# Products that nobody reads at every norm and around the last stage's routing

## The chip, the cores and the metric

The kernel runs on one core of one Trainium2 chip. The metric is the device time of one execution in microseconds; times of before are the median of three runs. TensorE (PE in the profile) multiplies, ScalarE (ACT) and VectorE (DVE) and GpSimd (POOL) work on tiles, SyncE (SP) issues most DMAs. TensorE's products land in PSUM, in tiles of one bank each: 512 f32 values in each of 128 partitions.

## The reference, cut to what matters

Three transformer blocks run one after the other on x of 256 tokens by 1024 features, in f32. What the change touches is the norms and the routing:

```python
def layer_norm(x, g, b):                       # first block, twice
    mu = mean(x, -1); var = mean((x - mu)**2, -1)
    return (x - mu) * rsqrt(var + 1e-5) * g + b
def rms_norm(x, g):                            # everywhere else
    return x * rsqrt(mean(x * x, -1) + 1e-6) * g

x = layer_norm(alpha * x + m @ w_out, ln1_g, ln1_b)        # first block, then its peer_ffn
x = layer_norm(alpha * h + f + e, ln2_g, ln2_b)
# second block, two layers: a mixer and an mlp, each output normed, scaled and added to x
x = x + rms_norm(mixer(rms_norm(x, g0)), g1)
x = x + rms_norm(mlp(rms_norm(x, g2)), g3)
# third block: mLSTM, SwiGLU, hgrn, mixture of experts, each behind a modulated rms_norm; a final rms_norm
top_logits, top_idx = top_k(t @ router_w, 2)               # the routing
top_w = softmax(top_logits)
y = sum over e of gates[:, e:e+1] * swiglu(t, wg[e], wu[e], wd[e])
```

## The kernel before

x stays in SBUF as a tile of 128 partitions by 8 slices by 256 tokens: features lie on partitions (slice k holds features 128k to 128k+127), tokens on the free axis. Every large product is made of three products of two-part values (`mm3`, lines L330 to L332): weights arrive by DMA, ACT rounds them to a part `hi` (L319) and DVE takes the rest `lo` (L320); inputs are split alike into pairs such as `nhi`, `nlo`. One such product is 128x256, in the trace as `128*128 128x256`, and its results gather in PSUM tiles named `mm` and `ac`. There are three pools of PSUM tiles: `mm` (two banks), `ac` (four) and `ms` (two); `ms` serves the norms and other small things.

A norm goes in a chain over several engines:

- Squares: ACT squares x by pairs of slices (L560, L564), DVE or POOL adds the tiles up (L568). The result is two tiles `sq`.
- `fold` (L497) multiplies them with a column of ones on TensorE: eight f32 products 128x1, in the trace 16 records of L371, into a bank `ms` ("the sums").
- `rstd` (from L373): ACT takes the root from that bank (`rs_t`, L379), DVE reads the same bank (`rs_v`, L380) and makes the reciprocal root in four more steps on 128x2 tiles (`rs_r`, L381 to L384).
- `rstd_rows` (L402) calls `spread` (L389): two f32 products 128x128 with the identity (four records of L394) put the 256 values on every partition, into the other bank `ms`.
- A reader takes the spread: DVE's `yk` in `layer_norm` (L456) and `rms` (L418), ACT's copy `rsb` in `add_normed` (L478), DVE's `x` at the end (L1987). From there ACT makes the rounded part (`lhi` L457, `nhi` L422 or L494), and the next stage's wide products can begin.

The norms are called at eleven places: twice `layer_norm` (first block); `add_normed` four times (second block: three times with `g`, where it prepares the next stage's input as well, and once without); `rms` through `modulated` three times in the third block (mLSTM, SwiGLU, hgrn); `Router.finish` for the routing (it uses `fold` and `rstd` but not `rstd_rows`); and the final norm (L1987). Where x is centred for a layer norm, its mean comes from `rows_add` (L400), f32 products 128x256.

The routing (`Router.finish` and `places`): ACT copies the logits to SBUF, TensorE transposes them (two products, L1795), DVE forms `lg` (L1797), takes the top values and their places (L1816, L1817), the masks `mk` (L1821); TensorE counts (L1824, L1825 and, for the largest count, L1840); DVE makes slots and the selectors `pm` (L1876); TensorE gathers the tokens of an expert (L1883), and the experts' products follow (L1908 on). Beside this chain, DVE and ACT make the normed tokens `xt` (L1804) and their parts `xhi`, `xlo` (L325, L326).

The program is written in order, and a scheduler places each engine's instructions; an instruction waits by semaphores for those on other engines whose tiles it needs.

Of the kernel before, what the change touches and what calls it, by code (L numbers as in the profile page):

```python
# [22 lines left out]
T = 256  # L23
# [194 lines left out]
class Core:  # L218
# [180 lines left out]

        self.nc.tensor.matmul(ps, self.C("onesD"), x, start=first, stop=last)  # L400

    def rstd_rows(self, sums, eps):  # L402
        return self.spread(self.ms_ps()[:, :T], self.rstd(sums[:, :2], eps))

    def squares(self, x):
        s = Squares(self)
# [1 line left out]
            s.add(x[:, 2 * j:2 * j + 2])  # L408
        return s

    def rms(self, x, sums, g, b=None, eps=1e-6):

        nc = self.nc
        r = self.rstd_rows(self.fold(sums), eps)
        hi, lo = self.big([KT, T], F32R, nm="nhi"), self.big([KT, T], F32R, nm="nlo")
        for k in range(KT):
            y = self.small([T], tag="yk", bufs=3)
            nc.vector.scalar_tensor_tensor(y, x[:, k], g[:, k:k + 1], r, op0=OP.mult, op1=OP.mult)  # L418
            if b is None:
                self.split(y, hi[:, k], lo[:, k])  # L420
            else:
                nc.scalar.activation(hi[:, k], y, AF.Identity, bias=b[:, k:k + 1])  # L422
                nc.vector.scalar_tensor_tensor(lo[:, k], y, b[:, k:k + 1], hi[:, k], op0=OP.add, op1=OP.subtract)
        return hi, lo
# [11 lines left out]
    def layer_norm(self, r, mean, g, b, g_next=None):  # L436


        nc = self.nc
        sq = Squares(self, nc.vector)  # L440
        for k in range(KT):
            nc.vector.tensor_tensor(r[:, k], r[:, k], mean, op=OP.subtract)
            if k % 2:
                sq.add(r[:, k - 1:k + 1])
        gh, bh = g, b
        if g_next is not None:
            gh, bh = (self.small([KT], tag=t, bufs=1) for t in ("gh", "bh"))
            nc.gpsimd.tensor_tensor(gh, g, g_next, op=OP.mult)
            nc.gpsimd.tensor_tensor(bh, b, g_next, op=OP.mult)
        rs = self.rstd_rows(self.fold(sq), 1e-5)  # L450
        hi, lo = (self.big([KT, T], F32R, nm="lhi"), self.big([KT, T], F32R, nm="llo"))
        sq = Squares(self)
        for k in range(KT):
            y = self.small([T], tag="yk", bufs=3)
            c = slice(k, k + 1)
            nc.vector.tensor_tensor(y, r[:, k], rs, op=OP.mult)  # L456
            nc.scalar.activation(hi[:, k], y, AF.Identity, scale=gh[:, c], bias=bh[:, c])  # L457
            eng = nc.vector if k < LNV else nc.gpsimd
            eng.tensor_scalar(r[:, k], y, g[:, c], b[:, c], op0=OP.mult, op1=OP.add)
            if g_next is None:  # L460
                nc.vector.tensor_tensor(lo[:, k], r[:, k], hi[:, k], op=OP.subtract)
            else:
                nc.vector.scalar_tensor_tensor(lo[:, k], r[:, k], g_next[:, c], hi[:, k], op0=OP.mult, op1=OP.subtract)
                if k % 2:
                    sq.add(r[:, k - 1:k + 1])
        return sq, (hi, lo)
# [4 lines left out]
    def add_normed(self, x, src, gm, sq, g=None):  # L471

        nc = self.nc
        r = self.rstd_rows(self.fold(sq), 1e-6)
        rs = self.small([T], tag="rsb", bufs=1)
        nc.scalar.activation(rs, r, AF.Copy)  # L478
        nxt = Squares(self, None if g is not None else nc.vector)
        parts = (self.big([KT, T], F32R, nm="nhi"), self.big([KT, T], F32R, nm="nlo")) if g is not None else None  # L480
        for k in range(KT):
            m = self.small([T], tag="yk", bufs=3)
            nc.vector.scalar_tensor_tensor(m, src(k), gm[:, k:k + 1], rs, op0=OP.mult, op1=OP.mult)
            eng = nc.vector if k < ADDS else nc.gpsimd
            eng.tensor_tensor(x[:, k], x[:, k], m, op=OP.add)
            if g is not None:
                self.scaled(x, k, g, parts)
            if k % 2:
                nxt.add(x[:, k - 1:k + 1])
        return nxt, parts  # L490
# [3 lines left out]
        self.nc.scalar.activation(hi, x[:, k], AF.Copy, scale=g[:, k:k + 1])  # L494
        self.nc.vector.scalar_tensor_tensor(lo, x[:, k], g[:, k:k + 1], hi, op0=OP.mult, op1=OP.subtract)  # L495

    def fold(self, sq):  # L497

        ps = self.sums()
        n = len(sq.tiles)  # L500
        for i, t in enumerate(sq.tiles):
            for f in range(2):
                self.add_sum(ps, 0, t[:, f], i + f == 0, i == n - 1 and f == 1, square=False)
        return ps
# [906 lines left out]
        nc.vector.tensor_tensor(self.mod[:, l, o:o + 16], cols, c.V(f"ada_b{l}")[:, o:o + 16], op=OP.add)  # L1411


def modulated(c, x, sums, w, scale, shift, out=None):
    nc = c.nc
    g = c.small([KT], tag="mg")
    nc.vector.scalar_tensor_tensor(g, scale, 1.0, w, op0=OP.add, op1=OP.mult)
    if out is None:
        return c.rms(x, sums, g, shift)
    return c.rms_whole(x, sums, g, shift, out=out)  # L1420


# [207 lines left out]
def hgrn(c, x, sums, mod):  # L1630
# [2 lines left out]
    nc.scalar.dma_start(lev, d["levels"])  # L1633
    masks = lev[:, :1024].bitcast(I32).rearrange("p (a b) -> p a b", a=8)
    reset = lev[:, 1024:1280]
    hs = modulated(c, x, sums, c.V("n1w1"), mod[:, 1, 8:16], mod[:, 1, 0:8])
    f, q = c.big([KT, T], nm="hf"), c.big([KT, T], nm="hq")
    P = lambda j: c.lin_chunk(d["h_in"][j], hs)
    for j in range(4):
# [3 lines left out]
    for j in range(2):  # L1643
        w = slice(4 * j, 4 * j + 4)
# [76 lines left out]
    v, g = c.big([2, D], nm="hv"), c.big([KT, T], nm="hg")  # L1721
# [11 lines left out]
    sq = {}  # L1733
# [17 lines left out]
class Router:  # L1751
# [35 lines left out]
    def finish(self, sq):  # L1787
        c, nc = self.c, self.c.nc
        r = c.rstd(c.fold(sq)[:, :2], 1e-6)
        lt = c.small([T], tag="lt", bufs=1)  # L1790
        nc.scalar.activation(lt[:8], self.lg, AF.Copy)
        pt = c.ac_ps()[:, :16].rearrange("p (a e) -> p a e", a=2)
        lg = c.small([2, 8], tag="lg", bufs=1)
        for tt in range(2):
            nc.tensor.transpose(pt[:, tt], lt[:8, tt * 128:tt * 128 + 128], c.C("ident")[:8, :8])  # L1795
        for tt in range(2):
            nc.vector.scalar_tensor_tensor(lg[:, tt], pt[:, tt], r[:, tt:tt + 1], self.bias, op0=OP.mult, op1=OP.add)  # L1797
        found = places(c, lg)
        parts = (c.big([2, D], F32R, nm="xhi"), c.big([2, D], F32R, nm="xlo"))
        for tt in range(2):  # L1800
            for a in range(0, D, 512):
                w = slice(a, a + 512)
                t = self.xt[:, tt, w]
                nc.vector.scalar_tensor_tensor(t, t, r[:, tt:tt + 1], self.row[:, w], op0=OP.mult, op1=OP.add)  # L1804
                c.split(t, parts[0][:, tt, w], parts[1][:, tt, w])
        return parts, found


def places(c, lg):

    nc = c.nc
    top, tf, mk = (c.hold([2, 8], t) for t in ("top", "tf", "mk"))
    ti = c.hold([2, 8], "ti", U32)
    oh = c.hold([2, 2, 8], "oh")
    for tt in range(2):
        nc.vector.max(top[:, tt], lg[:, tt])  # L1816
        nc.vector.max_index(ti[:, tt], top[:, tt], lg[:, tt])  # L1817
    nc.vector.tensor_copy(tf, ti)
    nc.vector.tensor_tensor(oh, c.C("iota")[:, None, None, :8].to_broadcast([128, 2, 2, 8]),
                            tf[:, :, 0:2, None].to_broadcast([128, 2, 2, 8]), op=OP.is_equal)  # L1820
    nc.vector.tensor_tensor(mk, oh[:, :, 0], oh[:, :, 1], op=OP.add)  # L1821
    ps = c.ms_ps()[:, :32]
    both = mk.rearrange("p a e -> p (a e)")
    nc.tensor.matmul(ps[:, 0:16], c.C("upto"), both, start=True, stop=False, skip_group_check=True)  # L1824
    nc.tensor.matmul(ps[:, 8:16], c.C("one"), mk[:, 0], start=False, stop=True, skip_group_check=True)  # L1825
    slot, gt = (c.hold([2, 8], t) for t in ("slot", "gt"))
    nc.vector.tensor_tensor(slot, mk, ps[:, 0:16].rearrange("p (a e) -> p a e", a=2), op=OP.mult)
    nc.vector.tensor_scalar(slot, slot, -1.0, None, op0=OP.add)

    w = c.hold([2, 4], "w")  # L1830
    nc.vector.tensor_tensor(w[:, :, 1:2], top[:, :, 1:2], top[:, :, 0:1], op=OP.subtract)
    nc.scalar.activation(w[:, :, 1:2], w[:, :, 1:2], AF.Exp)
    nc.vector.tensor_scalar(w[:, :, 2:3], w[:, :, 1:2], 1.0, None, op0=OP.add)
    nc.vector.reciprocal(w[:, :, 0:1], w[:, :, 2:3])
    nc.vector.tensor_tensor(w[:, :, 1:2], w[:, :, 1:2], w[:, :, 0:1], op=OP.mult)
    nc.vector.tensor_tensor(oh, oh, w[:, :, 0:2, None].to_broadcast([128, 2, 2, 8]), op=OP.mult)
    nc.vector.tensor_tensor(gt, oh[:, :, 0], oh[:, :, 1], op=OP.add)
    ps = c.ms_ps()[:, :8]
    for tt in range(2):
        nc.tensor.matmul(ps, c.C("one"), mk[:, tt], start=tt == 0, stop=tt == 1)  # L1840
    most = c.hold([1], "most")
    nc.vector.tensor_reduce(most, ps, axis=AX.X, op=OP.max)
    mosti = c.hold([1], "mosti", I32)
    nc.vector.tensor_copy(mosti, most)
    return slot, gt, mosti
# [177 lines left out]
```

## Time and profile before

| | us |
|---|---|
| median of three runs (lowest, highest) | 3037.54 (3036.64, 3039.58) |
| the profiled execution | 3037.25 |
| its span in the trace | 3035.1 |
| TensorE busy | 2847.2 (94%) |
| VectorE busy | 2120.3 (70%) |
| ScalarE busy | 1580.2 (52%) |
| GpSimd busy | 271.9 (9%) |
| mean granted clock of TensorE, share of full | 0.959 |

A row of a timeline gives the start and the duration of an instruction (or of several alike in a row, x16), both in us, its engine, its line, its operation with what it writes and reads, and in brackets how long the engine had been idle before it and whose work ended that. A busy time sums records; TensorE's records overlap, so a row of several gives their whole extent. PEclk is the granted clock as a share of full speed: 1.00 is 2.4 GHz and 0.50 is 1.2 GHz; a value between them is a mean over a stretch that has both.

### The profile page before, as it was taken

What the parts mean: (1) busy time and instruction counts of PE and PEld (TensorE: products, weight loads), DVE (VectorE), ACT (ScalarE), POOL (GpSimd) and SP (SyncE); (2) the same over time, 40 slices, a digit from 0 to 9 for tenths busy, and PEclk for the clock granted to TensorE, in tenths of its full rate; (3) what the DMA queues carried; (4) which work ended last, traced back from release to release, by engine and by line L of the source; (5) the groups of instructions that cost most, each with busy time, mean ns of one, the idle gap of its engine ahead of it and who ended that gap; (6) DMA issues with size and microseconds to landing.
All of it is one profiled execution on the core that took longest, in us unless ns stands there. A gap on an engine that the chain in (4) does not pass through costs nothing. (4 is left out here: it accounts for less than half of the span.)

```text
span 3035.1 us, 52257 instructions
## 1 busy us (share of the span) xinstructions
PE 2847.2 (94%) x21378; PEld 2707.3 (89%) x21378; DVE 2120.3 (70%) x3619; ACT 1580.2 (52%) x2233; POOL 271.9 (9%) x176
## 2 busy tenths in 40 slices
PE   8799967899999999999999999999999999999998
PEld 8698966899999999988799988999899998788886
DVE  6365998976666667577655655555655596899997
ACT  5254534654444444436644455445544565777775
POOL 0000372200000000021000100000100062000000
PEclk9899988999999999999999999998999999999999
DMA  7544333477877788443155423543245442688885
GB/s 260 180 149 159 142 124 128 170 274 287 289 263 280 280 292 305 170 144 128 56 182 188 145 99 139 181 168 139 85 167 183 160 141 97 249 316 336 321 333 220
DMA packets 117712, 601.77 MB, mean 198 GB/s; under 512 B 9688, under 2 KB 45016, under 8 KB 48472
## 3 DMA queue, kind: packets, MB, share of 16 engines
q1 hardware_dynamic: 78480, 557.96, 50.5%
q10 hardware_dynamic: 38984, 40.39, 4.4%
q8 instruction: 170, 2.79, 0.4%
q14 instruction: 78, 0.64, 0.1%
HBM read 578.91 MB, written 19.39 MB: 197 GB/s over the span
## 5 line engine op out<-in xcount | busy, mean ns | idle before, releaser
L320 DVE TENSOR_TENSOR lo<-raw,hi 128x1024 fp32r<-128x1024 f32 x915 | 1123.5, 1244 | 601.6 <-ACT hi L319 598.4
L319 ACT ACTIVATE hi<-raw 128x1024 fp32r<-128x1024 f32 x955 | 1002.7, 1057 | 1021.1 <-PE mm L331 534.1
L330 PE MATMUL mm<-lhi,hi 128*128 128x256 f32 x1344 | 388.2, 289 | 5.5 <-ACT r L930 3.1
L332 PE MATMUL mm<-lhi,lo 128*128 128x256 f32 x1344 | 388.1, 289 | 3.6 <-DVE lo L320 3.5
L330 PE MATMUL mm<-nhi,hi 128*128 128x256 f32 x1312 | 378.8, 290 | 10.2 <-ACT nhi L494 6.8
L331 PE MATMUL mm<-llo,hi 128*128 128x256 f32 x1344 | 388.2, 289 | 0.0
L331 PE MATMUL mm<-nlo,hi 128*128 128x256 f32 x1312 | 379.0, 289 | 0.5 <-DVE nlo L495 0.5
L332 PE MATMUL mm<-nhi,lo 128*128 128x256 f32 x1312 | 376.8, 288 | 0.0
L330 PE MATMUL ac<-r,hi 128*128 128x256 f32 x1024 | 294.2, 288 | 0.7 <-ACT r L325 0.7
L331 PE MATMUL ac<-r,hi 128*128 128x256 f32 x1024 | 293.4, 287 | 0.0
L332 PE MATMUL ac<-r,lo 128*128 128x256 f32 x1024 | 293.2, 286 | 0.0
L330 PEld LDWEIGHTS mm<-lhi,hi 128*128 128x128 f32 x1344 | 262.3, 195 | 7.9 <-ACT r L930 3.7
L330 PEld LDWEIGHTS mm<-nhi,hi 128*128 128x128 f32 x1312 | 258.0, 197 | 12.3 <-ACT nhi L494 7.6
L332 PEld LDWEIGHTS mm<-lhi,lo 128*128 128x128 f32 x1344 | 262.5, 195 | 5.7 <-DVE lo L320 4.7
L331 PEld LDWEIGHTS mm<-llo,hi 128*128 128x128 f32 x1344 | 262.2, 195 | 1.1 <-issue 0.7
L331 PEld LDWEIGHTS mm<-nlo,hi 128*128 128x128 f32 x1312 | 257.9, 197 | 2.5 <-DVE nlo L495 1.7
L332 PEld LDWEIGHTS mm<-nhi,lo 128*128 128x128 f32 x1312 | 257.8, 197 | 0.1
L330 PEld LDWEIGHTS ac<-r,hi 128*128 128x128 f32 x1024 | 198.8, 194 | 0.9 <-ACT r L325 0.9
L331 PEld LDWEIGHTS ac<-r,hi 128*128 128x128 f32 x1024 | 198.8, 194 | 0.0
L332 PEld LDWEIGHTS ac<-r,lo 128*128 128x128 f32 x1024 | 198.3, 194 | 0.0
L331 PE MATMUL ac<-hlo,hi 128*128 128x256 f32 x688 | 193.0, 281 | 0.0
L330 PE MATMUL ac<-hhi,hi 128*128 128x256 f32 x688 | 192.8, 280 | 0.0
(591 smaller groups left out, 6253.6 us busy)
## 6 DMA issues: line engine op xcount, KB each, us to landing
raw<-in_moe_gu SPq DMA_DIRECT2D x88, 1024.0 KB, 5.9
raw<-in_peer_u SPq DMA_DIRECT2D x64, 1024.0 KB, 5.3
raw<-in_peer_v SPq DMA_DIRECT2D x64, 1024.0 KB, 4.9
raw<-in_ada SPq DMA_DIRECT2D x48, 1024.0 KB, 6.1
raw<-in_moe_d SPq DMA_DIRECT2D x40, 1024.0 KB, 5.9
raw<-in_up SPq DMA_DIRECT2D x32, 1024.0 KB, 4.9
raw<-in_down SPq DMA_DIRECT2D x32, 1024.0 KB, 4.9
raw<-in_ffn_gu SPq DMA_DIRECT2D x22, 1024.0 KB, 4.9
```

Of the source, the lines that this page charges most:

```text
L319: nc.scalar.activation(hi, raw[:, a:a + m], AF.Copy)
L320: eng.tensor_tensor(lo, raw[:, a:a + m], hi, op=OP.subtract)
L330: mm(ps, w[0], x[0], start=start, stop=False, **k)
L331: mm(ps, w[0], x[1], start=False, stop=False, **k)
L332: mm(ps, w[1], x[0], start=False, stop=stop, **k)
```

## The change

A new helper `busy(ps, n)` makes n f32 products of the identity with the first 256 columns of the constants, into columns 256 to 511 of the bank `ps`. Nothing reads these columns. In the trace each is a product `128*128 128x256` in f32. It is called:

- in `rstd_rows`: three into the bank of the sums, behind `rstd`, and `more` into the spread's bank, behind the spread: three by default, five in `add_normed` with `g`, sixteen in `add_normed` without;
- in `fold`, ahead of its products, `wait` of them: nine in both layer norms, seven at the hgrn norm, none elsewhere;
- in `Router.finish`: nine behind the two transposes, in their bank; in `places`: five behind L1840's products, in their bank.

These are 118 products in all.

```diff
+    def busy(self, ps, n):
+        for _ in range(n):
+            self.nc.tensor.matmul(ps[:, 256:512], self.C("ident"), self.cst[:, 0:256], start=True, stop=True)
+
-    def rstd_rows(self, sums, eps):
-        return self.spread(self.ms_ps()[:, :T], self.rstd(sums[:, :2], eps))
+    def rstd_rows(self, sums, eps, more=3):
+        r = self.rstd(sums[:, :2], eps)
+        self.busy(sums, 3)
+        ps = self.ms_ps()
+        self.spread(ps[:, :T], r)
+        self.busy(ps, more)
+        return ps[:, :T]
...
-    def rms(self, x, sums, g, b=None, eps=1e-6):
+    def rms(self, x, sums, g, b=None, eps=1e-6, wait=0):
...
-        r = self.rstd_rows(self.fold(sums), eps)
+        r = self.rstd_rows(self.fold(sums, wait), eps)
...
-        rs = self.rstd_rows(self.fold(sq), 1e-5)
+        rs = self.rstd_rows(self.fold(sq, 9), 1e-5)
...
-        r = self.rstd_rows(self.fold(sq), 1e-6)
+        r = self.rstd_rows(self.fold(sq), 1e-6, 16 if g is None else 5)
...
-    def fold(self, sq):
+    def fold(self, sq, wait=0):
...
         ps = self.sums()
+        self.busy(ps, wait)
...
-    hs = modulated(c, x, sums, c.V("n1w1"), mod[:, 1, 8:16], mod[:, 1, 0:8])
+    hs = modulated(c, x, sums, c.V("n1w1"), mod[:, 1, 8:16], mod[:, 1, 0:8], wait=7)
...
-        pt = c.ac_ps()[:, :16].rearrange("p (a e) -> p a e", a=2)
+        bank = c.ac_ps()
+        pt = bank[:, :16].rearrange("p (a e) -> p a e", a=2)
...
             nc.tensor.transpose(pt[:, tt], lt[:8, tt * 128:tt * 128 + 128], c.C("ident")[:8, :8])
+        c.busy(bank, 9)
...
-    ps = c.ms_ps()[:, :8]
+    bank = c.ms_ps()
+    ps = bank[:, :8]
     for tt in range(2):
         nc.tensor.matmul(ps, c.C("one"), mk[:, tt], start=tt == 0, stop=tt == 1)
+    c.busy(bank, 5)
```

Below stands the scheduler's order at three places. The first is TensorE at the `add_normed` without `g`: L371 is the fold, L394 the spread, L406 the new products; `ms_` with a number is one bank's tile, and the brackets name the engines whose semaphores an instruction waits for. Before:

```order
L371 MATMUL ms_21417<-cst,sq_3037_21414 128x1 [waits Activation_49]
L371 MATMUL ms_21417<-cst,sq_3037_21414 128x1
L394 MATMUL ms_21426<-cst,rs_r_21428 128x128 [waits DVE_49]
L394 MATMUL ms_21426<-cst,rs_r_21428 128x128
L371 MATMUL ms_21483<-cst,sq_3046_21446 128x1 [waits DVE_49,PE_49]
```

With the change:

```order
L371 MATMUL ms_21471<-cst,sq_3037_21468 128x1 [waits Activation_49]
L371 MATMUL ms_21471<-cst,sq_3037_21468 128x1
L406 MATMUL ms_21471<-cst 128x256 [waits DVE_49]
L406 MATMUL ms_21471<-cst 128x256 x2
L394 MATMUL ms_21492<-cst,rs_r_21481 128x128 [waits DVE_49]
L394 MATMUL ms_21492<-cst,rs_r_21481 128x128
L406 MATMUL ms_21492<-cst 128x256 x16
L371 MATMUL ms_21556<-cst,sq_3046_21519 128x1 [waits DVE_49,PE_49]
```

Three products stand now between the last fold and the spread, in the fold's bank, the first of them with a wait for DVE; sixteen stand behind the spread, in its bank, ahead of the next norm's fold. At the other `add_normed` it is the same with five in place of sixteen. ACT's copy `rsb`, which reads the spread, waits for TensorE in both programs; its wait is set at the last of the sixteen (or five), where before it was set at the spread's last product.

The second place is TensorE at the SwiGLU norm, where products of the hgrn norm's call stand too (bank `ms_25287` is that of the hgrn norm's sums). Before:

```order
L371 MATMUL ms_23046<-cst,sq_3284_23037 128x1
L394 MATMUL ms_23055<-cst,rs_r_23057 128x128 [waits DVE_49,PE_49]
L394 MATMUL ms_23055<-cst,rs_r_23057 128x128
L330 MATMUL mm_23117<-nhi_23067,hi_23109 128x256 [waits Activation_49]
L330 MATMUL mm_23181<-nhi_23067,hi_23173 128x256
L331 MATMUL mm_23117<-nlo_23068,hi_23109 128x256 [waits DVE_49]
```

With the change:

```order
L371 MATMUL ms_23125<-cst,sq_3284_23116 128x1
L406 MATMUL ms_23125<-cst 128x256 [waits DVE_49]
L406 MATMUL ms_23125<-cst 128x256 x2
L394 MATMUL ms_23146<-cst,rs_r_23135 128x128 [waits DVE_49,PE_49]
L394 MATMUL ms_23146<-cst,rs_r_23135 128x128
L406 MATMUL ms_23146<-cst 128x256 x3
L406 MATMUL ms_25287<-cst 128x256 [waits PE_49]
L406 MATMUL ms_25287<-cst 128x256 x2
L330 MATMUL mm_23202<-nhi_23152,hi_23194 128x256 [waits Activation_49]
L330 MATMUL mm_23266<-nhi_23152,hi_23258 128x256
L406 MATMUL ms_25287<-cst 128x256
L331 MATMUL mm_23202<-nlo_23153,hi_23194 128x256 [waits DVE_49]
```

Behind the spread and its three products stand three of the seven that the hgrn norm's `fold` calls for, and a fourth after two wide products. The other three stand at the hgrn norm, right ahead of its fold.

The third place is DVE at the routing: `lg` are the logits (L1797 before, L1811 with the change), `mk` the masks (L1821, now L1835), `xt` and `xlo` the normed tokens and their second parts. Before:

```order
L1804 SCALAR_TENSOR_TENSOR xt_26640<-xt_26640,rs_r_26973,shift_26641 128x512 [waits DVE_49,Pool_49]
L1797 SCALAR_TENSOR_TENSOR lg_26984<-ac_26983,rs_r_26973,rbias_26663 128x8 [waits PE_49]
L1797 SCALAR_TENSOR_TENSOR lg_26984<-ac_26983,rs_r_26973,rbias_26663 128x8
L1816 MAX top_26989<-lg_26984 128x8 [waits DVE_49]
...
L1804 SCALAR_TENSOR_TENSOR xt_26640<-xt_26640,rs_r_26973,shift_26641 128x512
L1819 TENSOR_TENSOR oh_26993<-cst,tf_26990 128x32 [waits DVE_49]
L1804 SCALAR_TENSOR_TENSOR xt_26640<-xt_26640,rs_r_26973,shift_26641 128x512
L1821 TENSOR_TENSOR mk_26991<-oh_26993 128x16 [waits DVE_49]
```

With the change:

```order
L1818 SCALAR_TENSOR_TENSOR xt_26738<-xt_26738,rs_r_27071,shift_26739 128x512 [waits DVE_49,Pool_49]
L1818 SCALAR_TENSOR_TENSOR xt_26738<-xt_26738,rs_r_27071,shift_26739 128x512
L1818 SCALAR_TENSOR_TENSOR xt_26738<-xt_26738,rs_r_27071,shift_26739 128x512 [waits Activation_49]
L326 TENSOR_TENSOR xlo_27136<-xt_26738,xhi_27135 128x512 [waits PE_49,Activation_49]
L326 TENSOR_TENSOR xlo_27136<-xt_26738,xhi_27135 128x512 [waits Activation_49] x2
L1818 SCALAR_TENSOR_TENSOR xt_26738<-xt_26738,rs_r_27071,shift_26739 128x512
L1811 SCALAR_TENSOR_TENSOR lg_27082<-ac_27081,rs_r_27071,rbias_26761 128x8 [waits PE_49]
L1811 SCALAR_TENSOR_TENSOR lg_27082<-ac_27081,rs_r_27071,rbias_26761 128x8
L1830 MAX top_27096<-lg_27082 128x8 [waits DVE_49] x2
...
L326 TENSOR_TENSOR xlo_27136<-xt_26738,xhi_27135 128x512 [waits Activation_49]
L1832 CAST tf_27097<-ti_27099 128x16 [waits DVE_49]
L1833 TENSOR_TENSOR oh_27100<-cst,tf_27097 128x32 [waits DVE_49]
L1835 TENSOR_TENSOR mk_27098<-oh_27100 128x16 [waits DVE_49]
```

Before, one `xt` stood ahead of `lg`, and three `xt` and two `xlo` between `lg` and `mk`; now four `xt` and three `xlo` stand ahead of `lg`, and one `xlo` between the two. `lg` waits for TensorE in both; now its wait is set at the ninth of the new products behind the transposes.

## Rows read from the trace of the kernel before

**Rows 1.** The page's busy times of the engines (us, share of the span, instructions) and the granted clock of TensorE in 40 equal slices of the span, in tenths.

```profile
PE 2847.2 (94%) x21378; PEld 2707.3 (89%) x21378; DVE 2120.3 (70%) x3619; ACT 1580.2 (52%) x2233; POOL 271.9 (9%) x176
...
PEclk9899988999999999999999999998999999999999
```

**Rows 2.** The waits of TensorE over the whole span: which operation waited for whom, us in total, how many times, the longest in us.

```profile
PE ms L371 <- DVE sq L568: 18.2, 4, 7.3
PE ms L394 <- DVE rs_r L384: 13.3, 10, 2.2
```

**Rows 3.** The timeline of TensorE at the second layer norm: the means' products (L400), the fold (L371), the spread (L394); start and duration in us.

```profile
1308.44 3.62 PE L400 MATMUL ms<-x,cst 128*128 128x256 f32 x16
1315.98 2.50 PE L371 MATMUL ms<-cst,sq 128*128 128x1 f32 x16 [3.92 <-DVE sq L568]
1319.68 1.22 PE L394 MATMUL ms<-cst,rs_r 128*128 128x128 f32 x4 [1.20 <-DVE rs_r L384]
```

**Rows 4.** The timeline of all engines at the first `add_normed` with `g`; start and duration in us.

```profile
1496.09 1.05 PE L371 MATMUL ms<-cst,sq 128*128 128x1 f32 x8 [0.52 <-ACT sq L560]
...
1497.47 0.16 DVE L380 TENSOR_SCALAR rs_v<-ms 128x2 f32<-128x2 f32 x1 [0.45 <-ACT rs_t L379]
...
1498.35 1.22 PE L394 MATMUL ms<-cst,rs_r 128*128 128x128 f32 x4 [1.21 <-DVE rs_r L384]
1499.61 0.38 ACT L478 ACTIVATE rsb<-ms 128x256 f32<-128x256 f32 x1 [2.16 <-PE ms L394]
...
1501.83 0.58 PE L330 MATMUL mm<-nhi,hi 128*128 128x256 f32 x1 [2.27 <-ACT nhi L494]
```

**Rows 5.** Stretches of TensorE: from and to in us, length, busy us and instructions, granted clock, share of the DMA engines and GB/s. First three places where the new products go (behind `rs_v` at the first and the third `add_normed` with `g`, and at the final norm), then the stretches of wide products behind the first and the second layer norm, the second `add_normed`, the mLSTM norm, the SwiGLU norm, the hgrn norm, and the gather behind the routing.

```profile
1497.70:1499.60 1.90, 1.22 (x4) 0.59 0.82 224
1841.10:1842.50 1.40, 0.71 (x4) 1.00 0.74 164
3026.90:3028.70 1.80, 1.19 (x4) 0.50 0.00 0
300.00:303.30 3.30, 3.30 (x14) 0.50 0.00 0
1322.10:1327.30 5.20, 5.20 (x23) 0.50 0.00 2
1699.70:1702.80 3.10, 3.10 (x14) 0.50 0.00 0
2058.40:2064.60 6.20, 6.20 (x28) 0.50 0.00 0
2204.50:2208.00 3.50, 3.50 (x15) 0.50 0.12 52
2403.30:2409.30 6.00, 6.00 (x27) 0.50 0.42 162
2593.20:2597.10 3.90, 3.90 (x18) 0.50 0.00 0
```

**Rows 6.** The timelines of all engines at the other three `add_normed` (second and third with `g`, the one without): their spreads.

```profile
1696.16 1.22 PE L394 MATMUL ms<-cst,rs_r 128*128 128x128 f32 x4 [1.20 <-DVE rs_r L384]
...
1841.77 0.71 PE L394 MATMUL ms<-cst,rs_r 128*128 128x128 f32 x4 [1.21 <-DVE rs_r L384]
...
2043.08 0.71 PE L394 MATMUL ms<-cst,rs_r 128*128 128x128 f32 x4 [2.15 <-DVE rs_r L384]
```

**Rows 7.** The timelines of TensorE at the folds of the first layer norm, the mLSTM norm, the SwiGLU norm (its second half, and the first wide product behind that norm) and the hgrn norm.

```profile
292.97 3.46 PE L371 MATMUL ms<-cst,sq 128*128 128x1 f32 x16 [3.98 <-DVE sq L568]
...
2051.10 3.54 PE L371 MATMUL ms<-cst,sq 128*128 128x1 f32 x16 [7.32 <-DVE sq L568]
...
2199.79 1.05 PE L371 MATMUL ms<-cst,sq 128*128 128x1 f32 x8 [1.06 <-ACT sq L560]
...
2204.44 0.79 PE L330 MATMUL mm<-nhi,hi 128*128 128x256 f32 x2 [1.11 <-ACT nhi L422]
...
2396.15 3.54 PE L371 MATMUL ms<-cst,sq 128*128 128x1 f32 x16 [3.03 <-DVE sq L568]
```

**Rows 8.** The timelines of TensorE some 10 us behind the first and the third `add_normed` with `g`, at the next fold there.

```profile
1510.30 1.05 PE L371 MATMUL ms<-cst,sq 128*128 128x1 f32 x8 [0.44 <-POOL sq L568]
...
1854.22 0.94 PE L371 MATMUL ms<-cst,sq 128*128 128x1 f32 x7 [1.98 <-POOL sq L568]
```

**Rows 9.** The timeline of TensorE at the routing: the transposes of the logits and the first products of the gather.

```profile
2584.36 0.38 PE L1795 MATMUL ac<-cst,lt 8*128 8x8 f32 x2
...
2593.17 0.77 PE L1883 MATMUL ac<-pm,xhi 128*128 128x256 f32 x2 [2.17 <-DVE pm L1876]
```

**Rows 10.** The timeline of DVE at the routing.

```profile
2584.78 0.36 DVE L1797 SCALAR_TENSOR_TENSOR lg<-ac,rs_r,rbias 128x8 f32<-128x8 f32 x2 [0.49 <-PE ac L1795]
...
2587.47 0.75 DVE L1804 SCALAR_TENSOR_TENSOR xt<-xt,rs_r,shift 128x512 f32<-128x512 f32 x1
...
2588.90 0.17 DVE L1821 TENSOR_TENSOR mk<-oh 128x16 f32<-128x16 f32 x1
```

**Rows 11.** The chain of waits that ended last, in order of time: start and duration in us, what; here the fold and the spread of the final norm.

```profile
3022.73 3.59 PE ms L371 x16
...
3027.51 1.24 PE ms L394 x4
```

More of the change, by code (lines that the diff above doesn't have):

```diff
@@ L1411, in finish, with modulated @@
         nc.vector.tensor_tensor(self.mod[:, l, o:o + 16], cols, c.V(f"ada_b{l}")[:, o:o + 16], op=OP.add)
-def modulated(c, x, sums, w, scale, shift, out=None):
+def modulated(c, x, sums, w, scale, shift, out=None, wait=0):
     nc = c.nc
@@ L1418, in modulated @@
     if out is None:
-        return c.rms(x, sums, g, shift)
+        return c.rms(x, sums, g, shift, wait=wait)
     return c.rms_whole(x, sums, g, shift, out=out)
```

## The prediction, made before the changed kernel ran

> **What bounds the kernel now.** I read the page's shares first, then the waits of TensorE, then the timelines of the places that the diff touches. TensorE is busy for 94% of the span, and its granted clock is at full speed in most slices [rows 1]. So time is won or lost in two ways only: TensorE stands still, or it runs at its lower level. The norms are where both happen. The ten waits of the spread (L394) for DVE's `rs_r` are 13.3 us together, and the fold's four waits (L371) for DVE's `sq` are 18.2 us [rows 2]. A norm is a serial chain: fold, ACT and DVE on 128x2 tiles, spread, a reader of the spread (ACT's `rsb` or DVE's `yk`), ACT's `nhi`, and only then wide products. At the first norm of the two-mixer block, `rs_v` ends at 1497.63, the spread starts at 1498.35 and takes 1.22 us, `rsb` starts 0.04 us after it, and TensorE has its next wide product at 1501.83, after 2.27 us idle [rows 4]. **What stands between the spread and its reader is therefore on the path in full.** One more thing is in these rows: `rs_v` waits 0.45 us for ACT's `rs_t`, though both only read the bank of the sums and take nothing from each other [rows 4]. In this kernel two engines that touch one PSUM bank are put in order, whatever columns they touch.
>
> The clock falls in the norms' waits. It was 0.50 (1.2 GHz) in seven stretches right behind a norm or the routing, with TensorE busy throughout; they lasted 3.3, 5.2, 3.1, 6.2, 3.5, 6.0 and 3.9 us, and then it was at 2.4 GHz [rows 5]. A slow stretch costs half its length, so these cost 1.65, 2.6, 1.55, 3.1, 1.75, 3.0 and 1.95 us. That is all that a kept clock could give back behind these places.
>
> **The price of one unread product.** The rows have its shape: L400 is eight f32 products 128x256 (two records each), 3.62 us [rows 3], so 0.43 us each at the full clock. At 1.2 GHz no row shows it; I take twice that.
>
> **Part 1: three products in the sums' bank, n behind the spread.** The three can start once `rs_v` has read the bank, and the spread comes behind them: 3 x 0.43 = 1.30 us, where 0.72 us pass now [rows 4]. That is 0.58 us late. The spread then runs at 0.71 us, as where the clock is at 1.00 [rows 5, 6], and not at 1.22: 0.51 earlier where it was slow. The n products behind it are in the reader's bank and stand ahead of the reader in the program; in the built order the reader's wait is set at the last of them. So the reader is late by 0.07 + 0.43n where the spread was slow, and by 0.58 + 0.43n where it was fast:
> - n = 3 (two layer norms, three pre-norms of the last stage, final norm): 1.37 us;
> - n = 5 (three add_normed with g): 2.2 us in the first two, 2.75 in the third, whose spread is at 0.71 already [rows 6];
> - n = 16 (add_normed without g): 0.58 + 6.9 = 7.5 us. Here the reader heads a chain over DVE to the next fold, which TensorE awaits for 7.32 us [rows 7]; nothing else is there to hide it.
>
> The Trainium skill ("PSUM — Partial Sum Buffer", section "PSUM bank collisions raise a hardware error") says that the scheduler orders any two engines on one bank, disjoint columns included. That speaks against putting the products where the reader reads; by it the late readers above hold, and without it the sum would be the second rival's. The 0.45 us of `rs_v` agree.
>
> **Part 2: products ahead of the fold.** Nine at each layer norm take 9 x 0.43 = 3.9 us; the folds there wait 3.98 and 3.92 us for `sq` [rows 3, 7]: hidden, just. With the clock gone they would be up to 3.9 us late. Of the hgrn norm's seven the built order puts three ahead of its fold (1.3 us in 3.03 us of waiting [rows 7]) and four some 1,600 rows earlier, behind the SwiGLU norm's spread. There the wide products wait 1.11 us for `nhi` [rows 7] and three take 1.3: 0.2 late. What is gained: a fold of 16 at the full clock takes twice the 1.05 us of eight [rows 7], 2.1 us for 3.46 (first layer norm, -1.4) and 2.50 (second, -0.4); for hgrn's 3.54 I take -0.4, since three products may not bring the clock up.
>
> **Part 3: the wide products behind.** If they run at 2.4 GHz from their start, they give back -1.65 and -2.6 (layer norms), -3.1 (mLSTM), -1.75 (SwiGLU) and -3.0 (hgrn) [rows 5]. Behind add_normed with g there is nothing to win: TensorE later waits for POOL's `sq` anyway, 0.44 us behind the first and 1.98 us behind the third [rows 8], and POOL's chain starts from the late reader.
>
> **Part 4: routing.** Nine products stand between the transposes (L1795) and `lg`, which waits for all nine: 3.9 us. The built order uses that time: the other three `xt` (0.75 us each) and three `xlo` go ahead of `lg`. Three `xt` and two `xlo` lie now in the 4.1 us from `lg` to `mk` [rows 10], one `xlo` is left; so some 2.1 us remain there. So `mk` is 1.9 us late; the five products behind the counts (2.2 us) lie in the 2.17 us that the gather waits for `pm` [rows 9]; and the gather's slow 3.9 us become 1.95 [rows 5]. Together about +0.3 at the full clock.
>
> **Part 5: what the products cost at the low clock.** At the full clock the terms are: layer norms -1.7 and -1.65, add_normed +2.2, +2.2, +2.75 and +7.5, mLSTM -1.75, SwiGLU -0.2, hgrn -2.05, routing +0.3, final norm +1.4: **+9.0 us**. But a slow stretch need not vanish, it can move from the wide products onto the unread ones, and there it costs the same half. It costs nothing at best and 3.1 us at each of the eleven places at most (the longest stretch [rows 5]). I take 1.95, half of the middle one (3.9), where the norm finds the clock at 0.50 or falling late into it: mLSTM, SwiGLU, hgrn, routing, final norm (0.50 from its fold on [rows 5, 11]). I take half of that, 1.0, at the layer norms, where nine products run ahead; two thirds, 1.3, at the first two add_normed (0.59 [rows 5], the spread as slow in the second [rows 6]); a third, 0.6, at the other two, whose spreads run at 0.71 [rows 6]. The terms become -0.7, -0.65, +3.5, +3.5, +3.35, +8.1, +0.2, +1.75, -0.1, +2.25, +3.35: **+24.5 us**.
>
> The sum stands on the profiled execution, 3037.25 us (span 3035.1), which is 0.3 below the median of 3037.54. So I predict 3037.25 + 24.5, about **3061.8 us**.
>
> **Rivals.**
> 1. *The products cost no clock.* The same late readers, but TensorE stays at 2.4 GHz through every norm: +9.0, 3046.3 us. For it: less idle time than before in every norm. Against: long waits remain (the fold's 7.32 us [rows 7], `nhi` behind the reader), and the clock fell to 0.59 within a norm whose fold of eight had taken the short 1.05 us just before [rows 4, 5].
> 2. *Other side: the reader isn't held.* If the reader starts when the spread is done, and the products only fill waiting time, then the gains stand alone: wide products -12.1, folds -2.2, gather -1.95, against +0.07 to +0.58 a spread (+1.7 in all) and 0.2: -14.3, **3023.0 us**. It decides at each norm by one number, the time from the last record of the spread to the reader: 0.04 us as now [rows 4], or 0.43n. Against it: the order by bank that `rs_v` shows [rows 4], and the built order's waits. The Trainium skill ("TensorE: Matmul & The Clock Gate", section "HAM oscillation — how this bites in real kernels") says that waits between groups of products bring the clock down and each group then starts cold, which is what the seven stretches show; by that rule alone the change would give this rival's 3023.0.
> 3. *The slow stretch lies under the products everywhere*, at its longest: +9.0 + 11 x 3.1 = +43, 3080 us. For it: most products come behind idle time, and in the final norm the clock is 0.50 throughout [rows 5]. Against: four of the seven stretches are under 4 us.
> 4. *Nothing shows.* Holding costs and clock gains cancel to within 0.2%, about 6 us, which is what a measurement of this kernel can tell from no change. It needs half the readers free and the clock kept.
>
> **How the numbers follow.** The forecast has 0.62, the first rival 0.13, the second 0.05, the third 0.17, the fourth 0.03. Faster by over 0.2%: 0.05. Within: 0.03. Slower: 0.92. The range starts a little above the first rival and ends a little below the third, 3048 to 3076; what lies outside is most of the second and fourth and parts of the first and third, about 2 in 10. By far the largest single term is the sixteen products of add_normed without g; alone it is 7.5 us of 24.5.
>
> **What would show it.** Right: `rsb` in the first add_normed starts some 3.5 us later after `rs_v` than 1.98; in the one without g some 8 us later; TensorE's share rises while the time does too; the wide products behind mLSTM and hgrn run at 1.00. `lg` starts about 5 us after its transposes and DVE has `xt` and `xlo` ahead of it. Wrong: a reader that starts 0.04 us after the spread; or a stretch behind a norm still at 0.50 for 6 us, as then the products bought no clock at all and the sum goes towards the third rival; or products that run in less than 0.43 us.

## The result

The change is slower: 3068.28 us, median of five runs (3060.54 to 3076.78), against 3039.58 (3036.64 to 3050.13) for before; the ratio is 1.0092, interval 1.0064 to 1.0119. That is +28 us (20 to 36) where +24.5 was forecast, 3068 for 3061.8. The profiled execution took 3071.7 us, its span is 3069.6.

### The profile page after: what moved, and what is told of

Its sections match the earlier page's. It is cut to its first block, busy times and chain, and to the rows that moved or that the text cites. A ratio compares the mean times of both kernels' runs of the same rounds, so it can differ in the third digit from the quotient of the medians.

```text
span 3069.6 us, 52722 instructions
## 1 busy us (share of the span) xinstructions
PE 2901.1 (95%) x21614; PEld 2748.3 (90%) x21614; DVE 2121.0 (69%) x3619; ACT 1579.1 (51%) x2233; POOL 269.1 (9%) x176
```

## The profile after

The page's busy times and clock slices, in the same columns as [rows 1]:

```profile
PE 2901.1 (95%) x21614; PEld 2748.3 (90%) x21614; DVE 2121.0 (69%) x3619; ACT 1579.1 (51%) x2233; POOL 269.1 (9%) x176
...
PEclk9899978999999999999999999999999999999999
```

TensorE is busy for 54 us more, with a better clock (mean 0.966 for 0.959), and the time is longer: busy is not useful here.

The first `add_normed` with g, all engines, against [rows 4] (L394 is the spread, L406 the new products, L489 the copy `rsb`):

```profile
1493.80 0.16 DVE L380 TENSOR_SCALAR rs_v<-ms 128x2 f32<-128x2 f32 x1 [0.45 <-ACT rs_t L379]
...
1494.02 2.33 PE L406 MATMUL ms<-cst 128*128 128x256 f32 x6 [0.55 <-DVE rs_v L380]
...
1496.14 1.06 PE L394 MATMUL ms<-cst,rs_r 128*128 128x128 f32 x4
...
1497.00 2.86 PE L406 MATMUL ms<-cst 128*128 128x256 f32 x10
1499.89 0.38 ACT L489 ACTIVATE rsb<-ms 128x256 f32<-128x256 f32 x1 [6.12 <-PE ms L406]
...
1502.12 0.38 PE L330 MATMUL mm<-nhi,hi 128*128 128x256 f32 x1 [2.26 <-ACT nhi L505]
```

`rsb` has a new releaser: L406, not L394. It starts 2.7 us behind the spread's last record (1497.20), 0.03 us behind the last of the five products, and 5.9 us behind `rs_v`. The wait for `nhi` behind it is 2.26 us, where it was 2.27, so TensorE still stands still there.

The `add_normed` without g and the next fold, TensorE, against [rows 6, 7]; then ACT there:

```profile
2059.25 1.06 PE L394 MATMUL ms<-cst,rs_r 128*128 128x128 f32 x4
2060.10 7.65 PE L406 MATMUL ms<-cst 128*128 128x256 f32 x32
...
2075.07 3.54 PE L371 MATMUL ms<-cst,sq 128*128 128x1 f32 x16 [7.32 <-DVE sq L580]
```

```profile
2067.79 0.38 ACT L489 ACTIVATE rsb<-ms 128x256 f32<-128x256 f32 x1 [11.82 <-PE ms L406]
```

The sixteen hold `rsb` from 2060.31 to 2067.79, 7.5 us. The wait for `sq` behind them is 7.32 us, as before to the digit: they stand in front of the idle time instead of in it, and the fold behind it is slow again (3.54 us).

Stretches of TensorE in the columns of [rows 5]: the wide products behind the first and the second `add_normed` with g and the second layer norm, each with the stretch that follows it, then those behind the mLSTM, SwiGLU and hgrn norms, and the start of the gather:

```profile
1502.20:1511.50 9.30, 5.52 (x36) 1.00 0.01 2
1511.80:1521.90 10.10, 10.10 (x49) 0.50 0.00 0
1707.20:1716.40 9.20, 6.65 (x49) 1.00 0.04 5
1716.60:1726.70 10.10, 10.10 (x47) 0.50 0.26 98
1315.50:1327.30 11.80, 9.80 (x75) 1.00 0.06 10
1327.50:1334.10 6.60, 6.60 (x31) 0.50 0.38 124
2086.60:2098.00 11.40, 11.27 (x90) 1.00 0.01 2
2235.50:2247.00 11.50, 11.50 (x89) 1.00 0.00 0
2435.50:2450.00 14.50, 14.30 (x115) 1.00 0.20 68
...
2626.10:2627.80 1.70, 1.70 (x9) 0.50 0.00 0
```

All six runs of wide products behind norms start at 1.00 now, and there the change does what it says; the gather still starts at 0.50. But behind three of the six the clock falls again, for 6.6 to 10.1 us. Before, the first `add_normed` had its slow stretch at the start of the wide products, and none behind it:

```profile
1501.90:1508.20 6.30, 6.04 (x24) 0.50 0.00 0
1508.40:1520.00 11.60, 10.75 (x89) 1.00 0.08 20
```

What stands ahead of the three new slow stretches, on TensorE's timeline:

```profile
1326.15 0.39 PE L331 MATMUL mm<-llo,hi 128*128 128x256 f32 x1 [1.63 <-DVE llo L474]
...
1511.58 1.12 PE L371 MATMUL ms<-cst,sq 128*128 128x1 f32 x5 [1.97 <-POOL sq L580]
...
1716.53 0.80 PE L371 MATMUL ms<-cst,sq 128*128 128x1 f32 x3 [1.95 <-POOL sq L580]
```

TensorE is out of inputs: it waits 1.6 to 2 us for DVE's `llo` or POOL's `sq` (before, not at all at the first of these places, 0.44 us at the second [rows 8] and 0.76 at the third), and the next stretch is slow. A faster TensorE is only part of the reason; the inputs come later, too. At the first `add_normed` the fold needs the second of two `sq` that POOL makes. POOL and DVE there, first before, then with the change:

```profile
1508.97 1.28 POOL L568 TENSOR_TENSOR sq<-sq,sq 128x512 f32<-128x512 f32 x1
...
1509.38 1.95 DVE L320 TENSOR_TENSOR lo<-raw,hi 128x1024 fp32r<-128x1024 f32 x1 [0.58 <-ACT hi L319]
...
1509.18 1.23 DVE L320 TENSOR_TENSOR lo<-raw,hi 128x1024 fp32r<-128x1024 f32 x1
...
1509.25 2.27 POOL L580 TENSOR_TENSOR sq<-sq,sq 128x512 f32<-128x512 f32 x1
```

Before, POOL starts first and takes 1.28 us; now DVE's `lo` starts 0.07 us ahead of it, and POOL takes 2.27. That is 1.0 of the 1.5 us by which the wait grew. At the second layer norm two `x` of DVE stand ahead of the `llo`; DVE before, then POOL and DVE with the change:

```profile
1328.37 0.73 DVE L459 TENSOR_SCALAR x<-yk,vecs 128x256 f32<-128x256 f32 x2
...
1321.67 1.29 POOL L580 TENSOR_TENSOR sq<-sq,sq 128x512 f32<-128x512 f32 x1 [1.78 <-ACT sq L576]
...
1321.74 3.97 DVE L470 TENSOR_SCALAR x<-yk,vecs 128x256 f32<-128x256 f32 x2
...
1323.73 3.73 POOL L1004 MEMSET nq<- 64x2048 f32 x2
```

The two `x` take 3.97 us where they took 0.73, beside POOL's `sq` and its fills of `nq`; in before this `sq` came at 1330.27, behind them.

At the second layer norm the products ahead of the fold do their work: against [rows 3] the fold takes 1.95 us for 2.50 and the spread 0.61 for 1.22.

```profile
1304.47 4.05 PE L406 MATMUL ms<-cst 128*128 128x256 f32 x18
1308.46 1.95 PE L371 MATMUL ms<-cst,sq 128*128 128x1 f32 x16
1310.96 1.56 PE L406 MATMUL ms<-cst 128*128 128x256 f32 x6 [0.55 <-DVE rs_v L380]
1312.36 0.61 PE L394 MATMUL ms<-cst,rs_r 128*128 128x128 f32 x4
1312.80 1.46 PE L406 MATMUL ms<-cst 128*128 128x256 f32 x6
```

How much later the same wide product starts than in before, taken ahead of a place and 25 to 100 us behind it, gives what each place cost in the two profiled executions, in us. The last column reads the same from the kernel *none at sixteen* (below), which is the change but for the products behind the spread of the `add_normed` without g:

| place | forecast | read | read again |
|---|---|---|---|
| first layer norm | -0.7 | +0.4 | +0.4 |
| second layer norm | -0.65 | +3.8 | +3.8 |
| add_normed with g: first, second, third | +3.5, +3.5, +3.35 | +8.9, +7.2, +2.3 | +5.4, +4.0, +1.2 |
| add_normed without g, and mLSTM norm | +8.1, +0.2 | +11.0 | |
| SwiGLU norm | +1.75 | +3.2 | +1.7 |
| hgrn norm | -0.1 | -1.0 | +0.3 |
| routing | +2.25 | +1.4 | -0.2 |
| final norm | +3.35 | +2.9 | +4.1 |
| sum | +24.5 | +40.1 | |
| sum without the fourth row | +16.2 | +29.1 | +20.7 |
| between the two layer norms | 0 | -7.9 | -7.2 |
| elsewhere | 0 | +2.3 | +4.4 |

The -7.9 belongs to no edit (below), and one execution's place is good to some 4 us only, as the two columns show where the same products run.

## The experiments

Ratios are to before on the same chip, which had medians of 3034 to 3040 there. Diffs are to the change where nothing else is said.

**Reader free.**

```diff
-        self.busy(ps, more)
+        self.busy(sums, more)
```

> The change with one edit: the products behind the spread go into the bank of the sums, which nobody reads any more, instead of the spread's bank; their number and their place on TensorE stay. Theory (a reader that shares the bank waits for all of them): each reader starts within 0.1 us of the spread's end, at 2 to 3.7 us behind rs_v instead of 3.4 to 10.7; the products then fill the wait for nhi. In the changed kernel's trace they hold the readers for 2.2, 1.3, 2.7, 2.2, 2.2, 7.5, 2.5, 2.6, 1.6 and 1.3 us, 26 us in all: some 24 us faster than the change, 3044. Rival (TensorE's own time for them is the cost, wherever they stand): within 5 us of the change, 3063 to 3068.

3041.62 us, ratio 1.0006 (0.9994 to 1.0018): 0.9% below the change, some 26 us. The products stand where they stood on TensorE, as many as before; only their bank differs. At the `add_normed` without g, TensorE and then ACT:

```profile
2049.58 1.06 PE L394 MATMUL ms<-cst,rs_r 128*128 128x128 f32 x4
2050.44 8.07 PE L406 MATMUL ms<-cst 128*128 128x256 f32 x32
2058.35 1.84 PE L371 MATMUL ms<-cst,sq 128*128 128x1 f32 x16
```

```profile
2050.68 0.38 ACT L489 ACTIVATE rsb<-ms 128x256 f32<-128x256 f32 x1 [3.95 <-PE ms L394]
```

`rsb` starts 0.04 us behind the spread, the sixteen fill the wait for `sq`, and the fold behind them takes 1.84 us instead of 3.54. All ten readers start 0.04 to 0.12 us behind their spreads in this trace. The held reader is shown, by the whole time and at this place. At the three `add_normed` with g the profile still has +13.0 us to before, between the change's two readings (18.4 and 10.6), so there the gain isn't shown by place.

**None behind the spread** (the line `self.busy(ps, more)` left out).

> The change without the products behind the spread; the three ahead of it, those ahead of the folds and those at the routing stay. Theory (they hold the readers, but they keep the clock for the wide products): the 26 us come back and slow stretches of 3 to 6 us return behind the layer norms and the three norms of the last block, 8 us: 3050, some 6 us above the kernel in which the reader is free. Rival (they don't matter for the clock): 3042 to 3044, the same as there.

3045.55 us, ratio 1.0028 (1.0015 to 1.0041): between the two. The products behind the spread cost 0.6% in the reader's bank (1.0092 against 1.0028), and in a bank of their own they may return 0.2% (1.0006; the intervals meet).

**Ahead of the folds alone** (all calls of `busy` but that in `fold` left out).

> The kernel before with the products ahead of the fold at the two layer norms and the hgrn norm alone (9, 9 and 7). Theory: the folds there run at the full clock, 1.4, 0.5 and up to 1.6 us sooner, nothing is held: 3036 to 3038, 2 to 4 us below before. Rival (TensorE, faster behind the norm, runs out of inputs and gives it back): 3039 to 3041, no change.

3033.84 us, ratio 0.9984 (0.9971 to 0.9997): about 5 us (1 to 9) faster than before, so the theory, and rather more than it said. In the profile the three places have -1.0, -2.0 and -1.4 us to before.

**None at sixteen** (`0 if g is None else 5`).

> The change with none in place of sixteen behind the spread of the add_normed without g. Theory: rsb there starts 7.5 us sooner and everything behind it too: 3061, 7.5 us below the change. Rival (the wait behind it only gets longer, or the clock that they kept is lost): under 4 us.

3057.37 us, ratio 1.0061 (1.0046 to 1.0076), 0.3% or 9 us below the change, with intervals that meet; from that `add_normed` past the mLSTM norm its profile has +2.2 us to before where the change has +11.0. The largest term of the sum had its size, by the profiles more surely than by the times.

**None ahead of the spread, reader free.**

```diff
-        self.busy(sums, 3)
...
-        self.busy(ps, more)
+        self.busy(sums, more, r[:, :1].to_broadcast([128, 128]))
```

> The kernel with the free reader (products behind the spread in the bank of the sums), now also without the three products ahead of the spread. The products behind it take rs_r as their stationary operand, so that none of them moves ahead of the spread. Theory (the three delay the spread: it started 1.45 us behind rs_v at the full clock and 2.78 us at the low one in that kernel, 0.72 in before; over the ten norms 14 us): the spread starts at 0.72 us again, some 11 us faster than with the free reader alone (3041.6), 3031. Rival (they pay for themselves by the clock that they keep): 3039 to 3043.

3029.61 us, ratio 0.9975 (0.9962 to 0.9987), and on another chip:

> The kernel with the free reader and none ahead of the spread once more, on another chip, since of the variants measured its interval alone with that of the folds' products lay below one, and only just. If it is faster than before: a ratio of 0.996 to 0.999. If the first measurement was luck: 0.999 to 1.001.

3034.37 us, ratio 0.9988 (0.9976 to 0.9999). Both intervals lie below one, the second only just. The first lies below that of the free reader alone (0.9994 to 1.0018), the second meets it: where the reader is free, the three ahead of the spread cost 0.2 to 0.3%. The edit gives the products behind the spread another operand, too; what that does by itself wasn't measured. This version is 4 to 8 us faster than before, and 32 to 36 faster than the change.

**Second wait filled** (to that kernel; the same at the fold of fox).

```diff
-            inv.append(c.inverse(c.fold(sq)))
+            inv.append(c.inverse(c.fold(sq, 4, x[:, 6])))
```

> The same as the kernel without products ahead of the spread, and at the next fold behind each add_normed with g (mlp twice, fox once), where TensorE waits for POOL, four unread products that take slice 6 of x. Theory (behind the norm TensorE, at the full clock, runs out of inputs, waits up to 2 us for POOL, and the clock falls again): the second slow stretches some 15 us behind these three norms go, 3 to 5 us each in the places where they stood: 4 to 8 us faster than without, 3023 to 3027. Rival (the clock falls there for another reason, or the four products take the time that they save): within 2 us of it, 3029 to 3033.

3032.27 us, ratio 0.9992 (0.9978 to 1.0006): the rival, no gain. TensorE's stretches behind the three `add_normed` with g, first in this kernel, 20 us from the first wide products on; then in the kernel without the fill, where the clock falls behind them:

```profile
1495.20:1515.00 19.80, 17.84 (x131) 1.00 0.15 54
1693.30:1713.00 19.70, 18.32 (x136) 1.00 0.20 61
1843.50:1863.00 19.50, 17.90 (x133) 1.00 0.15 55
```

```profile
1505.00:1511.90 6.90, 6.90 (x34) 0.51 0.01 2
...
1706.40:1709.80 3.40, 3.40 (x17) 0.50 0.04 12
...
1846.40:1856.60 10.20, 10.07 (x60) 0.67 0.01 2
```

The second slow stretches are gone, but over the three places the profiles have +3.0 and +3.2 us to before. The fill also moved the fold behind other products, so its own price isn't separated from that.

That the wait for POOL brings the stretch is shown for the long waits alone. In the other thirteen traces a slow stretch begins within 4 us of each of the 22 folds there that waited 1.95 to 1.99 us, and of 10 of the 16 that waited 0 to 0.81 us. At all 22, POOL's `sq` took 2.24 to 2.30 us behind a `lo` of DVE that had just begun, as in the change above: the theory's words, that TensorE runs out because it is at the full clock, are half of it.

**Without the routing's products** (to the kernel with none ahead of the spread).

> The kernel without products ahead of the spread, and without the fourteen at the routing. Theory (they hold lg and most of what they gain at the gather is lost): the place of the routing, from the transposes to the experts' first products, takes 1.3 us less, 3030. Rival (the gather's clock is worth more than lg's delay): 1 to 2 us more, 3032 to 3033. The times alone may not tell these apart; the profile's gather does: it runs at 0.50 for 3.9 us again by the theory.

3035.21 us, ratio 0.9990 (0.9976 to 1.0003): above both ranges, but not clear of the kernel with the products (0.9975 and 0.9988). The gather does what the theory said. TensorE from the gather's first product on, in the kernel with the products, then without:

```profile
2587.30:2591.00 3.70, 3.70 (x32) 1.00 0.00 0
...
2593.70:2597.40 3.70, 3.70 (x17) 0.50 0.00 0
```

**The routing's products alone.**

> The kernel before with the fourteen products at the routing alone. Theory: 1.3 to 2.3 us slower than before, 3041, all of it at the routing; everything ahead of it as in before, within what one execution differs from another. Rival (they pay): 3036 to 3039.

3036.11 us, ratio 0.9991 (0.9975 to 1.0007). Times don't settle the routing. In the profiles its place has +1.6 us to before with the products alone and -0.1 without them, next to the forecast's +2.25; a cost of that size is below what the times can tell. All traces together do tell: from the transposes to the experts' first product it takes 15.1 to 16.7 us in the nine with these products (mean 16.2) and 14.4 to 15.2 in the five without (14.7). The means put their cost at 1.5 us: the gather starts 2.3 to 3.3 us later, and a faster gather returns a part.

These runs explain the -7.9 between the layer norms. Up to the second layer norm this kernel without the routing is, instruction by instruction, the one with it: from the first wide product behind the first layer norm to that behind the second, their profiles have 1021.4 and 1010.8 us (before: 1022.1; the change: 1013.7). Executions of one program differ there by 10 us: TensorE is busy 6 us longer in the first of the two, with 16 slow stretches for 13, and idle 4 us longer.

**Few, free** (to the kernel without the routing's products: 1, 2 and 16 behind the spread for 3, 5 and 16).

> The kernel without products ahead of the spread and without those at the routing, with one in place of three behind the spread, two in place of five at add_normed with g, sixteen still without g; all in the bank of the sums, the reader free. Theory (with the reader free the products cost where they outlast the wait for nhi: with three at the low clock the first wide product came 1.96 us behind the reader instead of 1.11, with five 3.67 instead of 2.22): wide products start 1.1 and 2.2 us behind the reader again, 4 to 7 us faster than with three and five (3035.2), 3028 to 3031. Rival (fewer products keep less clock): 3034 to 3038.

3035.55 us, ratio 0.9996 (0.9982 to 1.0010). The wide products start 1.1 us behind the layer norms' readers and 2.2 behind those of `add_normed` with g, as said, and no time comes of it: the rival.

**Only in long waits** (the same with 0, 0 and 16).

> Products only in TensorE's long waits for sq: 9, 9 and 7 ahead of the folds and the sixteen behind add_normed without g, in the bank of the sums; none else. Theory (a product helps where TensorE has nothing to do for long and nobody waits for it): folds behind run at the full clock and the mLSTM norm with them, 3028 to 3032. Rival (the short waits have to be filled too): like the kernel with products ahead of the folds alone, 3034.

3034.39 us, ratio 0.9993 (0.9977 to 1.0009). It doesn't tell the two apart: the interval holds the gain of 0.16% that the products ahead of the folds had alone, and none. The mLSTM fold ran faster, as said (1.86 us for 3.54), but the clock fell again behind it: 0.50 until 2066.58, with wide products from 2060.46.

**The change without the three ahead of the spread.**

```diff
-        self.busy(sums, 3)
```

> The change without the three products ahead of the spread; the readers are held as in the change. Theory (the spread waits for them: it started 1.5 to 2.8 us behind rs_v, 0.72 in before, 15 us over the ten norms): 10 to 15 us faster than the change, 3053 to 3058. Rival (they only take the low clock upon themselves, and the products behind the spread, which hold the readers, run at it in their place): 0.58 us a norm, 5 to 7 us, 3061 to 3063.

3065.83 us, ratio 1.0101 (1.0080 to 1.0121): no faster than the change (1.0092), neither by the theory's 10 to 15 us nor by the rival's 5 to 7. In the trace the rival's way shows. The first `add_normed` with g:

```profile
1501.29 1.22 PE L394 MATMUL ms<-cst,rs_r 128*128 128x128 f32 x4 [1.21 <-DVE rs_r L384]
...
1502.31 4.47 PE L406 MATMUL ms<-cst 128*128 128x256 f32 x10
1506.82 0.38 ACT L488 ACTIVATE rsb<-ms 128x256 f32<-128x256 f32 x1 [6.43 <-PE ms L406]
```

The spread starts 0.72 us behind `rs_v` again, but the five behind it run at the low clock, 4.47 us for 2.86, and `rsb` comes 6.2 us behind `rs_v`, for 5.9 in the change. Here the slow stretch only moves to whoever stands next. Over the ten norms the readers start 6.2 us sooner behind `rs_v` than in the change, the rival's size; the times don't show these us.

## Why the prediction was right

The range held the time, the direction and the size were right, and the mechanism is shown: a reader that shares a bank with products nobody reads waits for the last of them. That +24.5 came so near +28 is in part luck: the terms that were off lie on both sides (too low at the second layer norm, too small a gain at the hgrn fold), and one profile's places are too rough to say by how much each.

- **Price of one product.** 0.43 us was forecast at the full clock and twice that at the low one. In the change the sixteen take 7.65 us mostly at the full clock; the five of the last experiment take 4.47, 0.89 each, at the low one. Right.
- **Held readers.** Forecast 21 us for 49 products, and more for the low clock; 26 us came back when the bank was another. Added up over the ten norms, the readers start 57.7 us behind `rs_v`, against 19.0 in before: 38.7 late, where parts 1 and 5 together have 36.5. Right. The Trainium skill ("PSUM — Partial Sum Buffer", section "PSUM bank collisions raise a hardware error") has a rule that fits, that the compiler back end's scheduler puts any two engines on one bank and quadrant in order, reads and writes alike. The trace agrees: the columns are disjoint, and `rsb` waited 7.5 us.
- **The three ahead of the spread.** Forecast at almost nothing on a slow norm: the spread 1.30 us behind `rs_v`, and faster. It started 1.45 to 2.78 us behind, and stayed slow in six of the ten norms (about 1.06 us), so the payment failed there; part 5's surcharge covers it in the sum, in another place than it was put. With held readers the times show no cost (ratio 1.0092 with, 1.0101 without); with free ones 0.2 to 0.3%.
- **Ahead of the folds.** Right, and too low at the hgrn norm: -0.4 us was taken for three products, and the fold took 1.95 us for 3.54.
- **The wide products' gain.** Behind the norms they ran at 1.00 from their start, as forecast. At the second layer norm this step failed: it was to give -2.6 us, and the place reads +3.8, twice. There DVE's `x` ran beside POOL, TensorE waited for `llo`, and the clock fell behind that. In the six of the fourteen traces where that happened the place reads +0.9 to +3.8, in the other eight, before among them, -2.0 to +0.6.
- **Behind add_normed with g.** The path was right: TensorE waits for POOL's `sq`, whose chain starts from the late reader. But the forecast took the chain's length as fixed. From the end of `rsb` to the end of POOL's second `sq` it is 10.2 to 10.3 us in the traces where that `sq` starts ahead of DVE's `lo`, and 11.1 to 11.3 where `lo` starts first. With the change the longer one came at the first two places, and behind it a slow stretch of 10 us (before had one of 6.3 us at the first, but ahead of the wait for POOL, of which 0.44 us were left). The terms of +3.5 read +8.9 and +7.2, and in the second reading +5.4 and +4.0: that they were too low is likely, and isn't shown. The first of these places reads +3.8 also in the kernel with products ahead of the folds alone, where nothing there is changed.
- **Routing.** In the change `lg` starts 4.1 us behind the transposes and `mk` 1.85 behind `lg`, close to 3.9 and 2.1. Part 4's own terms (1.9 late, nothing, -1.95) add up to zero and not to its +0.3. The five products behind the counts weren't hidden: they ran at the low clock, 4.6 us for 2.2, ahead of the gather, whose first 1.7 us were slow still. The surcharge covers that.
- **The other side.** The second rival forecast -14.3 us for a free reader, the products where they are. That kernel was measured: +1.8 us (ratio 1.0006), so waits filled that way return nothing. Without the three ahead of the spread, which it priced at +1.7 us, the products gave 4 to 8 (ratios 0.9975 and 0.9988), a quarter to a half of the rest; and those ahead of the folds alone gave 5 (0.9984), so what the others add isn't shown. The Trainium skill ("TensorE: Matmul & The Clock Gate", section "HAM oscillation — how this bites in real kernels") tells of the clock that falls in waits, which the stretches behind the long waits for POOL show, and not of the next wait that a faster TensorE reaches sooner.

What stays open: how the 28 us of the medians divide over the places, as one profile's places vary by some 4 us.

## What to carry to other kernels

Work that keeps an engine warm must not touch a bank (or tile) that the next reader needs: put it into one that nobody waits for, and look at the reader's releaser in the trace to see that it did. Put it where the engine waits long for something that it can't delay, ahead of a fold and not behind a spread. A gain in clock counts only as far as the inputs keep up: look for the next wait before adding it up. And an engine that runs sooner shifts the others against each other: see whether two of them, here DVE and POOL, then overlap and slow each other.

## What the runs showed of the hardware

DVE and POOL slow each other where these tiles are made, and the one that starts later takes longer. The fourteen traces have 42 places behind an `add_normed` with g. Where DVE's `lo` began 0.04 to 0.12 us ahead of POOL's `sq` (27 of them), `sq` took 2.24 to 2.31 us; in the others it took 1.27 to 1.29, and a `lo` that began while it ran took 1.87 to 2.26 us instead of 1.23.

The clock fell while unread products ran: in the change at the first `add_normed` they began at 1494.02, and the granted clock is 0.50 in the following row with TensorE busy throughout. How the clock falls differs between executions of one program; over the 1,020 us between the layer norms the time differs by 10 us.

```profile
1495.00:1498.00 3.00, 3.00 (x11) 0.50 0.80 320
```
